# The head of a two-layer decoder trunk: first weights on a second queue, a norm vector spread by products, the second tile's steps reordered

## The chip, the cores and the metric

The kernel runs on one core of one Trainium2 chip. The metric is the device time of one execution in microseconds (us), lower is better. All times and profile rows below are of the kernel before the change, unless said otherwise.

## The reference, cut to what matters

The program computes two layers of a decoder trunk in float32 on 512 positions of 1024 channels. Only the very first sub-layer matters here: the root-mean-square norm of the input, and the product of the result with the value columns of the first mixer's input projection.

```python
def rmsnorm(x, g):
    x32 = x.astype(jnp.float32)
    y = x32 * lax.rsqrt(jnp.mean(x32 * x32, axis=-1, keepdims=True) + EPS)
    return y.astype(x.dtype) * g

h = rmsnorm(x, g_mix_pre[0])
proj = h @ w_in
q, k, v, f_logit, b_gate, c_gate, u = jnp.split(proj, [i1, i2, i3, i4, i5, i6], axis=-1)
...
x = x + rmsnorm(y, g_mix_post[layer])
```

After it come attention, a gated convolution, a recurrent block, two cross attentions and two SwiGLU layers, all untouched by the change.

## The kernel before

**Products.** Each float32 product is made of three passes over float32r operands: both sides are split into a high part (a cast on ScalarE) and a low part (a subtraction on VectorE), and TensorE adds high x high, high x low and low x high. In the tile names, wh and wl are the two parts of a weight tile st, hTh and hTl those of the transposed activations.

**The head of `fox` (lines 1236 to 1325).** The 512 positions are four tiles x[0] to x[3] of 128 rows by 1024 channels. For each tile: `row_stats` (line 235) takes the sum of squares of both halves, `rstd` (line 222) turns it into a factor with two small VectorE operations (L224, L228) and a power on GpSimd (L232), `scaled` (line 253) multiplies tile, factor and norm vector g (L258, two halves h), and `put_T` (line 301) transposes each half with four TensorE instructions into one PSUM bank (L305), casts that bank into hTh (L314, ScalarE) and subtracts it into hTl (L315, VectorE). `mm_v(k0, t, which)` (line 1242) then adds two of the eight 128-channel blocks of tile t into the tile's accumulator: "h" is hTh x wh, "x" is hTl x wh, "w" is hTh x wl; each letter is two matmuls of 512 columns (L1249). The weights come in four loads of 512 KB, `raw[0]`, `raw[2]`, `raw[4]`, `raw[6]`; `whi_v` casts one (L1273, ScalarE), `wlo_v` subtracts it (L1276, VectorE).

**What sets the order.** Inside the `with tc.manual_schedule` block the order of TensorE, ScalarE and VectorE is the order of the program text; each engine works strictly through its own list, and semaphores make it wait. All large loads are issued by SyncE (queue SP), in the order x[0], grow, g1, raw[0], x[1], raw[2], raw[4], x[2], raw[6], x[3].

**The norm vector.** g has two halves. The first is one row, loaded into row 0 of a zeroed tile `grow` and spread over all partitions by a float32 product with a tile of ones (L1280); it stays in a PSUM bank. The second, `g1`, is loaded 128 times over by a broadcasting DMA (L1262). Both are read by `scaled` of all four tiles.

**PSUM.** There are eight banks: pool A's four are the accumulators of the four tiles, pool B's four serve everything else, and a tile takes a bank of its pool when one is free, that is when every instruction on the tile that held it is done:

```python
psA = ctx.enter_context(tc.tile_pool(name="psA", bufs=4, space=bass.MemoryType.PSUM))
psB = ctx.enter_context(tc.tile_pool(name="psB", bufs=4, space=bass.MemoryType.PSUM))
...
for hf in range(2):
    ps = bank()
    for j in range(4):
        nc.tensor.transpose(out=ps[:, j * P:(j + 1) * P], in_=hs[hf][:, j * P:(j + 1) * P], identity=ident)
```

**Filler.** `warm_up(n)` issues n transposes of the identity into a pool-B bank `warm` (L1236); nobody reads them. There are 13 at the start and 4 after L1280.

Of the kernel before, what the change touches and what calls it, by code (L numbers as in the profile page):

```python
# [8 lines left out]
F32 = mybir.dt.float32  # L9
F32R = mybir.dt.float32r  # L10
BF16 = mybir.dt.bfloat16
AF = mybir.ActivationFunctionType
ALU = mybir.AluOpType
PE = mybir.EngineType.PE

P = 128
SEQ = 512
D = 1024
# [5 lines left out]
FOXW = 512  # L24
# [6 lines left out]
WS = 4  # L31
MID = 3
WARM = 13
WARM2 = 4
WHI = 4
WLO = 4
EPS = 1e-6
# [5 lines left out]
def trunk_kernel(ctx: ExitStack, tc: tile.TileContext, a: dict, out: bass.AP):  # L43
# [4 lines left out]
    nc = tc.nc  # L48
# [5 lines left out]
    wst = ctx.enter_context(tc.tile_pool(name="wst", bufs=WS))  # L54
    wlo = ctx.enter_context(tc.tile_pool(name="wlo", bufs=WLO))
    whi = ctx.enter_context(tc.tile_pool(name="whi", bufs=WHI))
    gains = ctx.enter_context(tc.tile_pool(name="gains", bufs=GB))
# [9 lines left out]
    def bankB():  # L67
        return psB.tile([P, 512], F32, tag="B", name="bB")
# [4 lines left out]
    def sbuf(name, n=512):  # L73
        return sp.tile([P, 516], F32, tag="s", name=name)[:, :n]

    def f(ap):
        return ap.bitcast(F32)
# [7 lines left out]
        out=mask, in_=mask, compare_op=ALU.is_ge, fill=1e30, base=0,  # L85
        pattern=[[-1, P]], channel_multiplier=1,
    )
    junk = const.tile([P, 512], BF16, name="junk")
    grow = sbuf("grow")
    ones = sbuf("ones", P)  # L90
    nc.vector.memset(grow, 0.0)
    nc.vector.memset(ones, 1.0)
    nhalf = const.tile([P, 1], F32, name="nhalf")
    nc.gpsimd.memset(nhalf, -0.5)

# [1 line left out]
    x = [xpool.tile([P, D], F32, name=f"x{t}", tag=f"x{t}") for t in range(NT)]  # L97

    def load_x(t):
        nc.sync.dma_start(out=x[t], in_=a["x"][0, t * P:(t + 1) * P, :])  # L100
# [16 lines left out]
    def load_raw(w, k0, nk, c0, c):  # L117
        st = wst.tile([P, nk, c], F32, tag="st", name="st")
        pace(nc.sync.dma_start(
            out=st, in_=w.rearrange("(k p) n -> p k n", p=P)[:, k0:k0 + nk, c0:c0 + c]  # L120
        ))
        return st
# [17 lines left out]
    def pace(load):  # L140

        loads[0] += 1
        if loads[0] > 0 and loads[0] % (COPIES + 1) and copies:
            with tc.issue_after(load.ins):
                copies.pop(0)()
# [73 lines left out]
    def sumsq(src, acc):  # L219
        nc.scalar.activation(out=junk, in_=src, func=AF.Square, accum_out=acc)  # L220

    def rstd(st):

        nc.vector.tensor_scalar(  # L224
            out=st[:, 2:3], in0=st[:, 0:1], scalar1=1.0 / D, scalar2=EPS,
            op0=ALU.mult, op1=ALU.add,
        )
        nc.vector.scalar_tensor_tensor(  # L228
            out=st[:, 3:4], in0=st[:, 1:2], scalar=1.0 / D, in1=st[:, 2:3],
            op0=ALU.mult, op1=ALU.add,  # L230
        )
        pool[0] = nc.gpsimd.tensor_tensor(out=st[:, 4:5], in0=st[:, 3:4], in1=nhalf, op=ALU.pow).ins  # L232
        return st[:, 4:5]

    def stats(name):
        return tiny.tile([P, 8], F32, tag="st", name=name)

    def row_stats(xt, both=False):

        st = stats("pre")  # L240
        for hf in range(2):
            src = xt[:, hf * 512:(hf + 1) * 512]
            if both and hf:
                nc.vector.tensor_tensor_reduce(
                    out=sbuf("sq"), in0=src, in1=src, scale=1.0, scalar=0.0, op0=ALU.mult, op1=ALU.add,
                    accum_out=st[:, hf:hf + 1],
                )
            else:
                sumsq(src, st[:, hf:hf + 1])
        return rstd(st)  # L250
# [36 lines left out]
    def dst_T(hT, hf, t):  # L287
        if hT.hi:
            sl = slice(t * P, (t + 1) * P)
            return hT.ghi[hf][:, :, sl], hT.glo[hf][:, :, sl]  # L290
        q, c = hT.quads[hf][t // 2], t % 2 * P
        return q[:, :, c:c + P], q[:, :, 256 + c:256 + c + P]
# [8 lines left out]
    def put_T(hT, t, hs, bank=bankB):  # L301
# [3 lines that stand above are left out]
                nc.tensor.transpose(  # L305
                    out=ps[:, j * P:(j + 1) * P], in_=hs[hf][:, j * P:(j + 1) * P], identity=ident
                )
            v = ps.rearrange("p (k c) -> p k c", k=4)
            sl = slice(t * P, (t + 1) * P)
            if hT.raw:  # L310
                nc.scalar.copy(out=hT.raw[hf][:, :, sl], in_=v)
            hi, lo = dst_T(hT, hf, t)
            last = (
                nc.scalar.copy(out=hi, in_=v).ins,  # L314
                nc.vector.tensor_tensor(out=lo, in0=v, in1=f(hi), op=ALU.subtract).ins,  # L315
            )
        return last
# [904 lines left out]
    def fox(proj):  # L1222
        w = a["ab_w_in"][0]
# [10 lines left out]
        def warm_up(n):  # L1234
            for _ in range(n):
                nc.tensor.transpose(out=warm[:, 0:P], in_=ident, identity=ident)  # L1236
# [4 lines left out]
        def mm_v(k0, t, which="hxw"):  # L1241

            ts = slice(t * P, (t + 1) * P)
            wh, wl = wv[k0]
            for c in which:
                for kk in range(2):
                    k = k0 + kk
                    passes[t] += 1
                    nc.tensor.matmul(  # L1249
                        out=banks[t], lhsT=(hT.lo if c == "x" else hT.hi)[k][:, ts],  # L1250
                        rhs=(wl if c == "w" else wh)[:, kk, :], start=passes[t] == 1, stop=passes[t] == 3 * KT
                    )
            if passes[t] == 3 * KT:
                dst = vhl[t].rearrange("p (m s d) -> p m s d", s=4, d=64)
                src = banks[t].rearrange("p (m s d) -> p m s d", s=2, d=64)
                split_out(src, dst[:, :, 0::3, :], dst[:, :, 1:3, :])

        with tc.manual_schedule(engines={PE, mybir.EngineType.Activation, mybir.EngineType.DVE}):
            load_x(0)
            nc.sync.dma_start(out=grow[0:1], in_=a["g_mix_pre"][0:1, 0:512])  # L1260
            g1 = gains.tile([P, 512], F32, tag="gain", name="gain")
            nc.sync.dma_start(out=g1, in_=a["g_mix_pre"][0, 512:D].partition_broadcast(P))  # L1262
            raw = {}
            for k0, t in ((0, 1), (2, None), (4, 2), (6, 3)):
                raw[k0] = load_raw(w, k0, 2, 2 * FOXW, 512)
                if t:
                    load_x(t)

            def whi_v(k0):
                hi = whi.tile([P, 2, 512], F32R, tag="wh", name="wh")  # L1270
                lo = wlo.tile([P, 2, 512], F32R, tag="wl", name="wl")
                wv[k0] = hi, lo
                nc.scalar.copy(out=hi, in_=raw[k0])  # L1273

            def wlo_v(k0):
                nc.vector.tensor_tensor(out=wv[k0][1], in0=raw[k0], in1=f(wv[k0][0]), op=ALU.subtract)  # L1276

            nc.scalar.activation(out=junk[:, 0:1], in_=nhalf, func=AF.Square)
            g0 = bankB()
            nc.tensor.matmul(out=g0, lhsT=ones, rhs=grow, start=True, stop=True)  # L1280
            g = g0, g1
            warm_up(WARM2)
            r = row_stats(x[0], True)
            nc.vector.tensor_copy(out=identb, in_=ident)
            hs = scaled(x[0], g, r)
            whi_v(0)
            wlo_v(0)
            put_T(hT, 0, hs)
            mm_v(0, 0, "hwx")
            whi_v(2)  # L1290
            r = row_stats(x[1], True)
            wlo_v(2)
            mm_v(2, 0, "hx")
            hs = scaled(x[1], g, r)
            whi_v(4)
            mm_v(4, 0, "hx")
            put_T(hT, 1, hs)
            mm_v(2, 0, "w")
            r = row_stats(x[2])
            wlo_v(4)  # L1300
            mm_v(0, 1)
            mm_v(2, 1)
            hs = scaled(x[2], g, r)
            whi_v(6)
            wlo_v(6)
            mm_v(4, 1)
            put_T(hT, 2, hs)
            mm_v(4, 0, "w")
            r = row_stats(x[3])
            hs = scaled(x[3], g, r)  # L1310
            mm_v(6, 0)
            mm_v(6, 1)
            for k0 in range(0, KT - 2, 2):
                mm_v(k0, 2)
            put_T(hT, 3, hs)
            mm_v(KT - 2, 2)
            for k0 in range(0, KT, 2):
                mm_v(k0, 3)
# [4 lines left out]
        st = load_raw(w, 0, KT, 3 * FOXW, 32)  # L1323
# [3 lines left out]
        for k in range(KT):  # L1327
# [5 lines left out]
            out=z, in0=ps[0:H], scalar=bf, in1=e, op0=ALU.add, op1=ALU.add  # L1333
# [5 lines left out]
            out=z, in0=z, scalar=0.0, in1=e, op0=ALU.min, op1=ALU.subtract  # L1339
# [3 lines left out]
            out=e, data0=t1, data1=z, initial=0.0, op0=ALU.mult, op1=ALU.add  # L1343
# [305 lines left out]
```

## Time and profile before

| what | value |
|---|---|
| time, median of 3 runs | 1389.0 us (1388.88 the lowest, 5210.49 the highest) |
| the profiled execution's own time | 1390.62 us |
| its span, first to last instruction | 1388.8 us |
| TensorE matmul busy | 1376.7 us, 99% of the span |
| VectorE, ScalarE, GpSimd busy | 1111.4, 727.0, 111.3 us |
| mean granted TensorE clock | 0.997 |

The span is what the rows below divide up; the profiled execution's own time also holds what lies around the span. PE is TensorE's matmuls, PEld its weight loads, DVE VectorE, ACT ScalarE, POOL GpSimd, SP SyncE; a "q" behind a name is the sequencer that issues a DMA. The granted clock (PEclk) is a share of full speed: 1.00 is 2.4 GHz, 0.50 is 1.2 GHz.

### The profile page before, as it was taken

What the parts mean: (1) busy time and instruction counts of PE and PEld (TensorE: products, weight loads), DVE (VectorE), ACT (ScalarE), POOL (GpSimd) and SP (SyncE); (2) the same over time, 40 slices, a digit from 0 to 9 for tenths busy, and PEclk for the clock granted to TensorE, in tenths of its full rate; (3) what the DMA queues carried; (4) which work ended last, traced back from release to release, by engine and by line L of the source; (5) the groups of instructions that cost most, each with busy time, mean ns of one, the idle gap of its engine ahead of it and who ended that gap; (6) DMA issues with size and microseconds to landing.
All of it is one profiled execution on the core that took longest, in us unless ns stands there. A gap on an engine that the chain in (4) does not pass through costs nothing.

```text
span 1388.8 us, 21768 instructions
## 1 busy us (share of the span) xinstructions
PE 1376.7 (99%) x8416; PEld 1226.8 (88%) x8416; DVE 1111.4 (80%) x1801; ACT 727.0 (52%) x1190; POOL 111.3 (8%) x160
## 2 busy tenths in 40 slices
PE   8999999999999999999999999999999999999998
PEld 6778788988899999998889888988889999999886
DVE  5876677645589999989898999653558999999987
ACT  4344456434455444456575797453446444545664
POOL 1000002012010011000001000101200011000001
PEclk9999999999999999999999999999999999999999
DMA  7854452668424566667665657266812555666654
GB/s 225 265 163 147 154 167 76 198 158 167 100 92 133 142 175 170 172 217 233 197 218 180 222 183 240 76 193 159 168 61 92 168 152 156 171 173 232 205 188 144
DMA packets 155250, 233.62 MB, mean 168 GB/s; under 512 B 8477, under 2 KB 90497, under 8 KB 153866
## 3 DMA queue, kind: packets, MB, share of 16 engines
q1 hardware_dynamic: 134562, 179.99, 40.3%
q0 software_dynamic: 17072, 46.16, 15.2%
q10 hardware_dynamic: 3512, 6.08, 1.4%
q8 instruction: 66, 1.08, 0.3%
q14 instruction: 38, 0.31, 0.1%
HBM read 219.60 MB, written 58.74 MB: 200 GB/s over the span
## 4 chain that ended last, share of the span: by engine, by line
PE 95%; issue 3%; DMA 1%; ACT 0%; DVE 0%; POOL 0%; DVEq 0%; SPq 0%; POOLq 0%; ACTq 0%
PE bA L336 13%; PE bA L338 13%; PE bA L337 13%; PE bB L337 6%; PE bB L336 6%; PE bB L338 6%; PE bB L811 3%; PE bB L810 3%; PE bB L812 3%; PE bA L811 2%; PE bA L810 2%; PE bA L812 2%; PE bA L569 2%; PE bA L571 2%; PE bA L570 2%
## 5 line engine op out<-in xcount | busy, mean ns | idle before, releaser
L546 DVE TENSOR_TENSOR wl<-st,wh 128x1024 fp32r<-128x1024 f32 x108 | 131.6, 1222 | 96.6 <-ACT wh L545 95.4
L545 ACT CAST wh<-st 128x1024 fp32r<-128x1024 f32 x108 | 113.1, 1050 | 120.4 <-PE bA L337 70.2
L336 PE MATMUL bA<-hTh,wh 128*128 128x512 f32 (+1 forms) x448 | 171.4, 383 | 0.2 <-ACT hTh L314 0.2
L337 PE MATMUL bA<-hTl,wh 128*128 128x512 f32 (+1 forms) x448 | 167.8, 375 | 0.3 <-DVE hTl L315 0.3
L338 PE MATMUL bA<-hTh,wl 128*128 128x512 f32 (+1 forms) x448 | 168.0, 375 | 0.0
L437 ACT CAST wg<-wr 128x1024 fp32r<-128x1024 f32 x80 | 83.7, 1046 | 49.2 <-DVE wr L466 38.5
L776 ACT CAST wh<-st 128x1024 fp32r<-128x1024 f32 x76 | 74.9, 986 | 63.7 <-PE bA L812 27.0
L338 PEld LDWEIGHTS bA<-hTh,wl 128*128 128x128 f32 x448 | 84.3, 188 | 15.4
L438 DVE TENSOR_TENSOR wg<-wr,wg 128x1024 fp32r<-128x1024 f32 x80 | 97.2, 1215 | 0.0
L337 PEld LDWEIGHTS bA<-hTl,wh 128*128 128x128 f32 x448 | 84.5, 189 | 14.2 <-DVE hTl L315 0.5
L336 PEld LDWEIGHTS bA<-hTh,wh 128*128 128x128 f32 x448 | 84.5, 189 | 14.0 <-ACT hTh L314 0.5
L781 DVE TENSOR_TENSOR wl<-st,wh 128x1024 fp32r<-128x1024 f32 x76 | 86.2, 1134 | 10.1 <-ACT wh L776 10.1
L437 ACT CAST wh<-tt 128x1024 fp32r<-128x1024 f32 x40 | 42.1, 1052 | 61.5 <-DVE tt L466 61.5
L336 PE MATMUL bA<-hTq,wh 128*128 128x256 f32 x208 | 59.2, 284 | 0.0
L338 PE MATMUL bA<-hTq,wl 128*128 128x256 f32 x208 | 58.9, 283 | 0.0
L337 PE MATMUL bA<-hTq,wh 128*128 128x256 f32 x208 | 58.8, 283 | 0.0
L810 PE MATMUL bB<-wh,ya 128*128 128x512 f32 x148 | 57.6, 389 | 0.0
L811 PE MATMUL bB<-wl,ya 128*128 128x512 f32 x148 | 57.6, 389 | 0.0
L812 PE MATMUL bB<-wh,ya 128*128 128x512 f32 x148 | 57.6, 389 | 0.0
L756 DVE TENSOR_TENSOR ya<-yb,ya 128x512 fp32r<-128x512 f32 x84 | 53.4, 639 | 0.0
L810 PE MATMUL bA<-wh,ya 128*128 128x512 f32 x132 | 51.3, 389 | 0.0
L811 PE MATMUL bA<-wl,ya 128*128 128x512 f32 x132 | 51.3, 389 | 0.0
(380 smaller groups left out, 4433.3 us busy)
## 6 DMA issues: line engine op xcount, KB each, us to landing
wr<-in_w_ffn_gu_dram SPq DMA_DIRECT2D x80, 512.0 KB
st<-t SPq DMA_DIRECT2D x40, 512.0 KB
t<-in_w_ffn_down_dram SPq DMA_DIRECT2D x32, 512.0 KB
st<-in_w_xkv_dram SPq DMA_DIRECT2D x32, 512.0 KB
st<-in_w_ffn_down_dram SPq DMA_DIRECT2D x30, 512.0 KB
st<-in_ab_w_in_dram SPq DMA_DIRECT2D x24, 512.0 KB
y<-yr POOLq DMA_DIRECT2D x18, 512.0 KB, 4.1
t<-in_w_ffn_down_dram POOLq DMA_DIRECT2D x16, 512.0 KB, 8.9
```

The source lines that it names most:

```text
L336: nc.tensor.matmul(out=ps, lhsT=wh, rhs=xh, start=first, stop=False)
L337: nc.tensor.matmul(out=ps, lhsT=wh, rhs=xl, start=False, stop=False)
L338: nc.tensor.matmul(out=ps, lhsT=wl, rhs=xh, start=False, stop=last)
L437: return (lambda: nc.scalar.copy(out=to[0], in_=src), lambda: nc.vector.tensor_tensor(out=to[1], in0=src, in1=f(to[0]), op=ALU.subtract))
L438: lambda: nc.vector.tensor_tensor(out=to[1], in0=src, in1=f(to[0]), op=ALU.subtract))
L545: nc.scalar.copy(out=hi, in_=src)
L546: nc.vector.tensor_tensor(out=lo, in0=src, in1=f(hi), op=ALU.subtract)
L776: nc.scalar.copy(out=self.wt[s][0], in_=self.st[s])
L781: nc.vector.tensor_tensor(out=lo, in0=self.st[s], in1=f(hi), op=ALU.subtract)
L810: nc.tensor.matmul(out=banks[t], lhsT=yh, rhs=wh[:, jj, :], start=first and jj == 0, stop=False)
L811: nc.tensor.matmul(out=banks[t], lhsT=yh, rhs=wl[:, jj, :], start=False, stop=False)
L812: nc.tensor.matmul(out=banks[t], lhsT=yl, rhs=wh[:, jj, :], start=False, stop=last and jj == n - 1)
```

## The change

The load of `raw[0]` is issued by ScalarE's queue instead of SyncE's. Both halves of the norm vector are now loaded as single rows (row 0 and row 32 of `grow`), split into a high part `growh` (ScalarE) and a low part `growl` (VectorE), and spread by two float32r products each with `pick`, a tile of zeros and ones; both halves stay in pool-B banks, and the broadcasting load is gone. The ones tile is gone too. The second half of x[1]'s sum of squares moves ahead of `wlo_v(0)` on VectorE, its first half behind `put_T(hT, 0, hs)`, and its `rstd` ahead of `whi_v(2)`. Of the filler, 2 transposes instead of 4 follow the norm vector's products, and 3 new ones stand between `put_T(hT, 0, hs)` and the first `mm_v`. `load_raw`'s pacing hook is bypassed for these four loads; its counter is negative there and set to 0 behind the block.

```diff
--- before.py
+++ after.py
@@ -31,7 +31,8 @@
 WS = 4
 MID = 3
 WARM = 13
-WARM2 = 4
+WARM2 = 2
+WARM3 = 3
 WHI = 4
 WLO = 4
 EPS = 1e-6
@@ -87,9 +88,11 @@
     )
     junk = const.tile([P, 512], BF16, name="junk")
     grow = sbuf("grow")
-    ones = sbuf("ones", P)
+    growh, growl, pick = (gains.tile([P, 512], F32R, tag="gain", name=n) for n in ("growh", "growl", "pick"))
     nc.vector.memset(grow, 0.0)
-    nc.vector.memset(ones, 1.0)
+    nc.vector.memset(f(pick)[:, 0:2 * P], 0.0)
+    for hf in range(2):
+        nc.vector.memset(f(pick)[32 * hf:32 * hf + 1, hf * P:hf * P + P], 1.0)
     nhalf = const.tile([P, 1], F32, name="nhalf")
     nc.gpsimd.memset(nhalf, -0.5)
 
@@ -1257,14 +1260,16 @@
 
         with tc.manual_schedule(engines={PE, mybir.EngineType.Activation, mybir.EngineType.DVE}):
             load_x(0)
-            nc.sync.dma_start(out=grow[0:1], in_=a["g_mix_pre"][0:1, 0:512])
-            g1 = gains.tile([P, 512], F32, tag="gain", name="gain")
-            nc.sync.dma_start(out=g1, in_=a["g_mix_pre"][0, 512:D].partition_broadcast(P))
+            for hf in range(2):
+                nc.sync.dma_start(out=grow[32 * hf:32 * hf + 1], in_=a["g_mix_pre"][0:1, hf * 512:hf * 512 + 512])
+
             raw = {}
-            for k0, t in ((0, 1), (2, None), (4, 2), (6, 3)):
-                raw[k0] = load_raw(w, k0, 2, 2 * FOXW, 512)
+            for k0, engine, t in ((0, nc.scalar, 1), (2, nc.sync, None), (4, nc.sync, 2), (6, nc.sync, 3)):
+                raw[k0] = wst.tile([P, 2, 512], F32, tag="st", name="st")
+                engine.dma_start(out=raw[k0], in_=w.rearrange("(k p) n -> p k n", p=P)[:, k0:k0 + 2, 2 * FOXW:3 * FOXW])
                 if t:
                     load_x(t)
+            nc.scalar.activation(out=junk[:, 0:1], in_=nhalf, func=AF.Square)
 
             def whi_v(k0):
                 hi = whi.tile([P, 2, 512], F32R, tag="wh", name="wh")
@@ -1275,20 +1280,41 @@
             def wlo_v(k0):
                 nc.vector.tensor_tensor(out=wv[k0][1], in0=raw[k0], in1=f(wv[k0][0]), op=ALU.subtract)
 
-            nc.scalar.activation(out=junk[:, 0:1], in_=nhalf, func=AF.Square)
-            g0 = bankB()
-            nc.tensor.matmul(out=g0, lhsT=ones, rhs=grow, start=True, stop=True)
-            g = g0, g1
+
+            nc.scalar.copy(out=growh, in_=grow)
+            g = bankB(), bankB()
+            st = stats("pre")
+
+            def square_v(t, hf):
+                src = x[t][:, hf * 512:(hf + 1) * 512]
+                if hf:
+                    nc.vector.tensor_tensor_reduce(
+                        out=sbuf("sq"), in0=src, in1=src, scale=1.0, scalar=0.0, op0=ALU.mult, op1=ALU.add,
+                        accum_out=st[:, 1:2],
+                    )
+                else:
+                    sumsq(src, st[:, 0:1])
+
+            square_v(0, 1)
+            square_v(0, 0)
+            nc.vector.tensor_tensor(out=growl, in0=grow, in1=f(growh), op=ALU.subtract)
+            r = rstd(st)
+            for hf in range(2):
+                for i, part in enumerate((growh, growl)):
+                    nc.tensor.matmul(out=g[hf], lhsT=pick[:, hf * P:hf * P + P], rhs=part, start=i == 0, stop=i == 1)
             warm_up(WARM2)
-            r = row_stats(x[0], True)
             nc.vector.tensor_copy(out=identb, in_=ident)
             hs = scaled(x[0], g, r)
             whi_v(0)
+            st = stats("pre")
+            square_v(1, 1)
             wlo_v(0)
             put_T(hT, 0, hs)
+            warm_up(WARM3)
+            square_v(1, 0)
             mm_v(0, 0, "hwx")
+            r = rstd(st)
             whi_v(2)
-            r = row_stats(x[1], True)
             wlo_v(2)
             mm_v(2, 0, "hx")
             hs = scaled(x[1], g, r)
```

## Rows read from the trace of the kernel before

**Rows 1.** The page's first part: busy time and share of the span.

```profile
PE 1376.7 (99%) x8416; PEld 1226.8 (88%) x8416; DVE 1111.4 (80%) x1801; ACT 727.0 (52%) x1190; POOL 111.3 (8%) x160
```

**Rows 2.** Waits of TensorE's matmuls over the whole span, the longest three of six.

```profile
PE bA L1249 <- ACT hTh L314: 1.5, 1, 1.5
PE bB L1236 <- POOL ident masks.py:199: 1.5, 1, 1.5
PE bB L305 <- DVE h L258: 1.3, 1, 1.3
```

**Rows 3.** The chain that ended last, first 25 us: start, length, what.

```profile
2.19 7.46 DMA st<-in_ab_w_in_dram
...
11.25 6.27 PE bA L1249 x14
```

**Rows 4.** Timeline of TensorE: start, length, engine, line, tiles, shapes, count.

```profile
1.47 3.03 PE L1236 MATMUL bB<-ident 128*128 128x128 f32 x13 [1.47 <-POOL ident masks.py:199]
4.30 1.91 PE L1280 MATMUL bB<-grow,ones 128*128 128x512 f32 x2
...
7.14 0.66 PE L305 MATMUL bB<-ident,h 128*128 128x128 f32 x4
9.12 0.66 PE L305 MATMUL bB<-ident,h 128*128 128x128 f32 x4 [1.31 <-DVE h L258]
...
14.83 1.06 PE L1249 MATMUL bA<-wh,hTl 128*128 128x512 f32 x2
15.68 1.06 PE L1249 MATMUL bA<-wh,hTh 128*128 128x512 f32 x2
...
17.35 1.04 PE L305 MATMUL bB<-ident,h 128*128 128x128 f32 x8
...
20.39 0.61 PE L1249 MATMUL bA<-wh,hTh 128*128 128x512 f32 x2
20.84 0.62 PE L1249 MATMUL bA<-wh,hTl 128*128 128x512 f32 x2
```

**Rows 5.** Timeline of VectorE, ScalarE and GpSimd, the first tile's chain.

```profile
4.10 0.69 DVE L244 CUSTOM_DVE_ANT_0 sq<-x 128x512 f32<-128x512 f32 x1 [2.56 <-DMA x<-in_x_dram]
4.17 0.63 ACT L220 ACTIVATE junk<-x 128x512 bf16<-128x512 f32 x1 [1.30 <-DMA x<-in_x_dram]
...
5.43 0.56 POOL L232 TENSOR_TENSOR pre<-pre,nhalf 128x1 f32<-128x1 f32 x1 [3.71 <-DVE identb L1284]
...
6.34 0.75 DVE L258 SCALAR_TENSOR_TENSOR h<-x,pre,bB 128x512 f32<-128x512 f32 x1 [0.94 <-PE bB L1280]
...
8.31 0.75 DVE L258 SCALAR_TENSOR_TENSOR h<-x,pre,gain 128x512 f32<-128x512 f32 x1 [1.22 <-DMA gain<-in_g_mix_pre_dram]
...
9.67 1.04 ACT L1273 CAST wh<-st 128x1024 fp32r<-128x1024 f32 x1 [4.78 <-DMA st<-in_ab_w_in_dram]
10.62 1.07 ACT L314 CAST hTh<-bB 128x512 fp32r<-128x512 f32 x2
10.74 1.23 DVE L1276 TENSOR_TENSOR wl<-st,wh 128x1024 fp32r<-128x1024 f32 x1 [1.68 <-ACT wh L1273]
...
11.88 1.28 DVE L315 TENSOR_TENSOR hTl<-bB,hTh 128x512 fp32r<-128x512 f32 x2
...
13.08 0.68 DVE L244 CUSTOM_DVE_ANT_0 sq<-x 128x512 f32<-128x512 f32 x1
```

**Rows 6.** Windows: stretch, length, busy by engine, granted clock, DMA share, GB/s.

```profile
2.00:4.00 2.00, 2.00 (x11) 2.00 (x10) 0.00 (x0) 0.85 (x2) 0.00 (x0) 1.00 1.05 283
4.00:6.00 2.00, 2.00 (x5) 0.86 (x4) 1.15 (x5) 0.72 (x2) 0.56 (x1) 1.00 0.76 102
...
7.10:10.40 3.30, 1.31 (x8) 0.84 (x8) 0.75 (x1) 0.73 (x1) 0.00 (x0) 1.00 1.02 400
10.60:17.20 6.60, 5.95 (x14) 4.65 (x15) 5.74 (x10) 3.69 (x7) 1.47 (x1) 0.50 1.07 374
17.40:25.00 7.60, 7.57 (x41) 5.79 (x40) 5.43 (x9) 4.52 (x10) 1.46 (x1) 1.00 0.70 217
```

## The prediction

> **What bounds the kernel now.** I read the page's busy shares first: TensorE works 1376.7 us of the 1388.8 us span [rows 1], so only its idle time and its slow time can be won. The list of its waits says where the idle time is: 1.5 us before the first filler, 1.3 us before the second group of transposes, 1.5 us before the first V matmul, each once [rows 2]; the other three of that list are shorter. All three lie in the first 11.25 us. So whatever moves the point from which TensorE runs dense moves the end by as much, and nothing later swallows it. The chain of waits names what holds that point: the load of raw[0], from its issue at 2.19 to its landing at 9.65 [rows 3], then its cast on ScalarE (9.67, 1.04 us), the cast of the first hTh behind it on the same engine (10.62) [rows 5], and 14 matmuls from 11.25 on [rows 3]. Then I asked for the granted clock by stretches: 1.00 until 10.4, 0.50 from 10.6 to 17.2, 1.00 from 17.4 on [rows 6]; 0.50 is 1.2 GHz, 1.00 is 2.4 GHz. A pair of matmuls starts every 0.85 us in the slow stretch and every 0.45 us behind it [rows 4], 0.43 and 0.225 us a matmul. The first clock rows need care: fillers at 1.47 take 3.03/13 = 0.23 us each, the transposes at 17.35 take 1.04/8 = 0.13 [rows 4], so TensorE began at the low level whatever the 1.00 in the rows 2 to 6 us says.
>
> **Where I measure.** All 14 matmuls of the first tile (six of `mm_v(0, 0)`, four of `mm_v(2, 0)`, four of `mm_v(4, 0)`) stand ahead of the second tile's transposes in both kernels. Those start at 17.35 [rows 4]. I work out when they start after the change and call the difference the effect.
>
> **Loads.** The change removes the 128-fold load of g1, during which the DMA engines were 0.76 busy and moved only 102 GB/s from 4 to 6 us [rows 6], and takes raw[0] out of SP's row, where x[0], grow and g1 stood before it. In SP's row two rows of grow now stand between x[0] and x[1]. raw[0] and x[0] are then under way together. x[0] lands at 4.10 now [rows 5]. It can stay there (0), or wait until raw[0] is through as well: 0.52 MB more at 283 GB/s [rows 6] is 5.95 (+1.85). Below 0 I see nothing, as g1 stood behind it. I take 4.6 (+0.5), nearer to the low end, since half of x[0] is through before raw[0] starts. raw[0] lands near 5.95 (behind x[0] alone) or as late as 7.8 (x[1]'s 0.52 MB through first); x[1] between 6.7 (1.05 MB behind x[0] at 400 GB/s [rows 6]) and 8.7 (that and half of raw[2] at 283).
>
> The Trainium skill, "DMA: Bandwidth & Descriptors", section "Issuing engines are not separate DMA queues", speaks against this part: loads started by several engines share the same 16 DMA engines, and only issue time is saved. By that rule alone x[0] would be at the late end, and the sum below 0.7 us larger; the DMA share of 1.05 from 2 to 4 us [rows 6] agrees that there is no spare engine.
>
> **The norm vector.** Added: a cast of 128x512 on ScalarE, 1.07/2 = 0.53 us by the cast of hTh; a subtraction on VectorE, 1.28/2 = 0.64 by hTl [rows 5]; four products of 512 columns at 0.43. Gone: two products of L1280, 1.91 together [rows 4], and the wait of the second h for g1, 1.22 [rows 5]. On ScalarE the cast comes before the sum of squares: 4.6 + 0.53 + 0.63 = 5.76 (the row of grow may land up to 0.5 later or with x[0]; I take with it). From the end of that sum (4.80 now) to the power is 0.63, the power 0.56 [rows 5], so the factor is there at 6.95 and the two h run 7.0 to 7.75 and 7.75 to 8.5, against 9.06 now. growl is ready at 4.6 + 0.7 + 0.64 = 5.95, so the first half's product ends about 6.4, the second's at 7.3, and both are hidden; the cover is thin (0.45 us before the second h).
>
> **The first tile, where the gain is given back.** The old kernel had four pool-B banks for warm, g's first half and the first tile's two transposed halves. Now warm is still needed by the three new fillers behind `put_T`, and g holds two banks to the end of the block. One bank is left. The second half's transposes must wait until the first half has been cast and subtracted out of that bank, and that subtraction (hTl) is behind other work in VectorE's list: the second h (ends 8.5), the moved square of x[1] (0.68, to 9.2), `wlo_v(0)` (1.23, to 10.45; its cast is through by then, as raw[0] need only land by 8.1), hTl itself 0.64: 11.1. Queued behind the waiting transposes on TensorE is everything else. The first half's own transposes end near 8.7, so TensorE idles 2.4 us. From 11.1: four transposes and three fillers at 0.23 are 1.6 us, and the first V matmul starts at 12.7 (12.0 if they ran at 0.13), 1.45 us later than now. Everything that it needs is there, and raw[2]'s cast and the second tile's h (about 17) come in time.
>
> **The clock.** The dense stretch begins at 11.1 instead of 11.25, with the same kind of pause before it, so I leave the fall near 10.5 and the rise at 17.3. By 17.3, (17.3 - 12.7)/0.43 = 10.7 matmuls are through; the other 3.3 take 0.75 us: the second tile's transposes start at 18.05, 0.7 us later than now. (While the rise stays put, 1 us of later start costs only about 0.5, since what is lost was slow time.) Bounds: with x[0] at 4.10, start 12.2, +0.45; with x[0] at 5.95, start 14.05, +1.4.
>
> **The other edits.** x[1]'s moved halves and its `rstd` are the same instructions; their price is the 0.68 us above. Memsets on VectorE lie before x[0] lands. Two fillers fewer, three more: counted above. Behind 18.05 the lists are unchanged, and the later tiles' inputs come sooner than now: 0.
>
> **Sum.** The profiled execution takes 1390.62 (its span 1388.8 and 1.8 around it); plus 0.7 is 1391.3. It lies 1.6 above the median of the runs shown, so against that 1389.0 the forecast is 1389.7.
>
> **Rivals.**
> First, the bank doesn't block (a bank comes free that I count as held). For it: three new fillers in front of the first matmul would have a pause to fill only then. Against it: pool B has four banks and three have later readers. Then the second transposes run at 8.5 to 9.4, the fillers to 10.1, hTh is ready, low parts follow VectorE (wl 10.45, hTl 11.1), and TensorE is dense from 7.8 and so keeps the high level. The 14 matmuls then go at the pace of ScalarE's casts: raw[4]'s cast ends near 13, and the second h of x[1] near 15.2, so the transposes start around 15.1: -2.2 us, 1386.8.
> Second, the bank blocks but the clock rises earlier, near 14, the seven short instructions counting as part of the dense stretch. For it: the same short ones stood before the high level at 7.1. Against it: ahead of the last rise TensorE had been busy 5.95 of 6.60 us [rows 6], and the new dense stretch is no older at 14. Three matmuls slow and eleven at 0.225: transposes at 16.45, -0.9, 1388.1.
> The Trainium skill, "TensorE: Matmul & The Clock Gate", section "Part 4: PE-mode transpose", says that transposes don't count as busy work for the clock in the same way. By that rule this rival is out and 1389.7 stands; the fall of the clock behind a stretch that held only eight transposes, 1.31 us of 3.30 [rows 6], agrees, but no row has them dense and alone.
> Third, on the slow side: x[1] lands late. Its square now stands ahead of `wlo_v(0)` and hTl, so from a landing at 8.5 on each microsecond delays the blocked transposes by one. The trace bounds the landing by 13.08, where its square ran without a wait [rows 5]. Halfway, 10.8, the first matmul starts at 15.0 and the transposes at 19.2: +1.9, 1390.9; at the bound +3, 1392. For it: three loads now share the start. Against it: g1's slow stretch is gone.
>
> **How the numbers follow.** Forecast 0.5, bank free 0.2, earlier clock 0.18, late x[1] 0.12. The likeliest one's own range is 1389.1 to 1390.7 (the bounds of x[0], a little either side). To hold 8 in 10 over both signs I go from 1386.6 (first rival) to 1391.3 (third rival's nearer half). A measurement of this kernel can tell about 2%, 28 us, from no change; all idle and slow time of the head together is under 10 us, so same 0.98, and 0.01 for each side for a reordering elsewhere that I don't see.
>
> **What would show it.** Right: the second group of L305 starts 2 us or more after the first and is released by L315; L1249 starts near 12.7; the clock is 0.50 to about 17.3; raw[0]'s cast no longer waits for its load. Wrong: both groups of L305 lie together and L1249 starts at 10 to 11 (first rival); 1.00 from 14 on (second); L244's second instance waits for x (third).

## The result, and the profile after

| kernel | median, us | runs | ratio to before, 95% interval |
|---|---|---|---|
| before | 1389.25 | 17 | |
| after | 1391.99 | 17 | 1.0020 (1.0013 to 1.0028) |

The change costs 2.74 us. The forecast was +0.7 us, 1389.7, with a range up to 1391.3: the sign is right, the size is too small, and the time lies 0.7 us above the range. The profiled execution of after took 1392.30 us, its span is 1390.5, 1.7 more than before's.

The page's first line shows that TensorE is as busy as before over a longer span [rows 1], so the time went into waits or slow work:

```profile
PE 1376.0 (99%) x8419; PEld 1226.6 (88%) x8419; DVE 1112.4 (80%) x1804; ACT 727.4 (52%) x1191; POOL 110.2 (8%) x160
```

The waits of TensorE's matmuls, the longest four (in total, times, longest), beside [rows 2]:

```profile
PE bB L1304 <- ACT growh L1284: 2.3, 1, 2.3
PE bB L308 <- DVE hTl L318: 2.0, 1, 2.0
PE bB L1239 <- POOL ident masks.py:199: 1.5, 1, 1.5
PE bA L308 <- DVE h L261: 1.0, 1, 1.0
```

The second is the blocked bank of the forecast: transposes into pool B (bB) that wait for hTl. The first is the norm vector's row, the fourth was forecast by nobody: it writes a pool-A bank (bA), so it is not in the head at all, where pool A holds the accumulators. The chain that ended last tells the head in one piece (start, length, what), in the place of [rows 3]:

```profile
1.79 4.27 DMA grow<-in_g_mix_pre_dram
...
6.17 0.63 ACT growh L1284
...
6.81 0.69 DVE growl L1300
...
7.94 0.56 POOL pre L235
...
8.53 0.75 DVE h L261 x2
...
9.91 0.69 DVE sq L1291
...
10.60 1.14 DVE wl L1281
11.74 0.61 DVE hTl L318
...
12.40 0.66 PE bB L308 x4
13.06 0.33 PE bB L1239 x3
13.39 4.79 PE bA L1252 x14
```

Before, this chain ran through raw[0] and ScalarE; now it runs from the row of grow through VectorE: the second h, the moved square, raw[0]'s subtraction, hTl, and only then the second half's transposes, the three fillers and the 14 matmuls. TensorE's timeline, beside [rows 4], gives the points of the forecast:

```profile
9.43 0.96 PE L308 MATMUL bB<-ident,h 128*128 128x128 f32 x4
12.40 0.66 PE L308 MATMUL bB<-ident,h 128*128 128x128 f32 x4 [2.01 <-DVE hTl L318]
...
13.14 0.83 PE L1252 MATMUL bA<-wh,hTh 128*128 128x512 f32 x2
...
18.02 1.03 PE L308 MATMUL bB<-ident,h 128*128 128x128 f32 x8
```

First matmul at 13.14 (forecast 12.7, before 11.25), second tile's transposes at 18.02 (forecast 18.05, before 17.35). That last agreement is in part luck: the blocked transposes start 1.3 us later than forecast (12.40 against 11.1), but they and the three fillers take 0.74 us instead of the 1.6 of the forecast, and the low clock has ended by 17.0. Windows of the granted clock, beside [rows 6]:

```profile
13.60:16.90 3.30, 3.30 (x10) 2.38 (x9) 2.56 (x5) 2.58 (x5) 0.55 (x1) 0.50 0.61 180
17.00:20.00 3.00, 3.00 (x17) 2.12 (x16) 1.54 (x4) 1.35 (x3) 0.00 (x0) 1.00 0.79 248
```

So the head of these two executions differs by 0.67 us, but their spans by 1.7. The missing 1.0 us is the fourth wait, at the transposes of a later projection (timeline of TensorE, after):

```profile
232.28 0.39 PE L574 MATMUL bB<-rh,y 128*128 128x512 f32 x1
233.63 1.29 PE L308 MATMUL bA<-ident,h 128*128 128x128 f32 x8 [0.97 <-DVE h L261]
```

There VectorE was held by an hTl that waited for the store of memT, 1 MB that GpSimd sends to memory:

```profile
DVE hTl L318: 1.5, 1
...
DMA to landing us min/median/max: 6.1/6.1/6.1
```

### The profile page after: what moved, and what is told of

Read it like the earlier page. It is cut to its first block, busy times and chain, and to the rows that moved or that the text cites. A ratio compares the mean times of both kernels' runs of the same rounds, so it can differ in the third digit from the quotient of the medians.

```text
span 1390.5 us, 21779 instructions
## 1 busy us (share of the span) xinstructions
PE 1376.0 (99%) x8419; PEld 1226.6 (88%) x8419; DVE 1112.4 (80%) x1804; ACT 727.4 (52%) x1191; POOL 110.2 (8%) x160
## 4 chain that ended last, share of the span: by engine, by line
PE 94%; issue 3%; DMA 1%; DVE 1%; ACT 0%; POOL 0%; DVEq 0%; ACTq 0%; POOLq 0%; SPq 0%
PE bA L339 13%; PE bA L341 13%; PE bA L340 13%; PE bB L339 6%; PE bB L340 6%; PE bB L341 6%; PE bB L815 3%; PE bB L813 3%; PE bB L814 3%; PE bA L815 2%; PE bA L813 2%; PE bA L814 2%; PE bA L572 2%; PE bA L574 2%; PE bA L573 2%
```

## The experiments

My theory was now: (A) the loss is a blocked bank behind a late row, plus (B) an accident at 232 us. Every kernel was timed beside the kernel before, and each profile also shows the store of memT. The medians of the kernel before lie between 1389.19 and 1389.76 in these rounds, so a difference of two medians from different rounds is good to about half a microsecond; the same difference by the ratios to before is given beside it where it matters.

**The late wait: fewer fillers after, more before.** `fill10` and `before_fill16` change one constant, the number of fillers at the start. In the kernel after, TensorE idles behind them; in the kernel before, three more push the norm vector's product back, and yet the second tile's transposes start no later (15.71, against 17.35 in [rows 4]).

```diff
-WARM = 13
+WARM = 10
```
```diff
-WARM = 13
+WARM = 16
```

> The kernel after the change with 10 instead of 13 fillers at the start, where TensorE idles 2.3 us anyway. Theory A (late fetch): the 0.97 us wait of the transposes at 232.7 us comes from the store of memT sharing a DMA engine with a fetch of TensorE's instructions; three instruction pairs fewer let that fetch come about 0.7 us later, behind the store's tail. Then the wait is gone or much smaller, the head is as before, and the time is about 1 us less, 1391.0. Rival (the store is slow by itself, or by load traffic): the wait stays at about 1 us and the time at 1392.0.

> The kernel before the change with 16 instead of 13 fillers at the start. In the head they delay the norm vector's product by about 0.7 us, which the second h hides, as it waits for g1 until 8.3. Theory A (late fetch): three instruction pairs more bring the fetch of TensorE's instructions into the store of memT, a wait of about 1 us appears at the transposes near 232 us, 1390.3. Rival: nothing changes, 1389.3.

fill10: 1390.92 (ratio to before 1.0008, 0.9999 to 1.0016), 1.07 under after, 1.7 by the ratios. before_fill16: 1391.17 (1.0008, 0.9999 to 1.0017), 1.4 over the kernel before beside it, 1.1 by the ratio, whose interval only just holds no change; its profile has the new wait, 1.0 us for DVE h at the same transposes. What decides is in the DMA view of the same 4.1 us from the store's issue on; first after, then fill10:

```profile
q0 software_dynamic: 140, 1.02, 61.7%
q8 instruction: 1, 0.02, 1.5%
```
```profile
q0 software_dynamic: 143, 1.05, 62.8%
```

In after a 16 KB fetch of instructions falls into that stretch, and 140 packets of the store have started by its end; in fill10 the fetch comes later, 143 have started, and the store, issued at 224.8 as against 224.7, lands in 4.8 instead of 6.1 us:

```profile
DVE hTl L318: 0.2, 1
...
DMA to landing us min/median/max: 4.8/4.8/4.8
```

The same split runs through all fourteen profiles: the seven of programs with 8419 matmuls have a landing of 6.0 to 6.3 us, the seven of programs with 8416 one of 4.8 or 4.9. The change's three extra TensorE instruction pairs moved the fetch forward into the store. The packet records of the traces say more. In the seven profiles with the short landing the fetch starts 2 or 3 ns after the store's last packet ends. In the other seven it starts 1.9 to 4.6 us before that end, and the store's last packets end one after another, 0.31 us apart. That fits one DMA engine which both have to pass, though the records do not name the engine, nor whose instructions are fetched.

**The bank.** `bank_free` lets the three new fillers write a pool-A bank that is reset later, so warm's bank is free.

```diff
-            warm_up(WARM3)
+            warm_up(WARM3, banks[NT - 1])
```

> The kernel after the change, its three new fillers written into the last accumulator bank of pool A, so that the bank of warm is free for the first tile's second transposes. Theory (bank): the second group of transposes no longer waits for hTl but follows the second h at about 10.0, the first V matmul starts near 11.5 instead of 13.1, and the time is 0.8 to 1.6 us less, 1390.4 to 1391.2 (the wait near 232 us may stay). Rival (the low parts on VectorE hold the matmuls anyway): the transposes move but the second tile's transposes don't, and the time stays at 1392.

1390.26 (1.0005, 0.9996 to 1.0013), 1.73 under after, 2.1 by the ratios. All eight transposes now go in one piece, and the first matmul starts 1.8 us earlier (timeline of TensorE):

```profile
9.15 1.92 PE L308 MATMUL bB<-ident,h 128*128 128x128 f32 x8
...
11.36 1.06 PE L1252 MATMUL bA<-wh,hTh 128*128 128x512 f32 x2
```

**The bank and the fetch together.** `bank_fill10` is bank_free with `WARM = 10`.

> bank_free with 10 instead of 13 fillers at the start: the blocked bank and the late fetch repaired together, nothing else. Theory (the two are the whole loss): 1.7 and 1.1 us add up, 1389.1 to 1389.4, the same as the kernel before, with no wait near 232. Rival (the head's gain of bank_free is taken back by the wait near 75 us, or a third loss is left): 1389.8 or more.

1388.84 (ratio to before 0.9994, 0.9985 to 1.0002): 3.15 under after, 3.6 by the ratios, and no different from before. The two repairs account for the whole loss; what else the change does is too small to be told from nothing here. The wait near 75 us is 0.3 us, as in after; in bank_free it was 0.7.

**The row.** `grow_act` issues the two rows on ScalarE's queue, ahead of raw[0]; `raw0_sp` leaves them and takes raw[0] back to SyncE's queue.

```diff
-                nc.sync.dma_start(out=grow[32 * hf:32 * hf + 1], ...
+                nc.scalar.dma_start(out=grow[32 * hf:32 * hf + 1], ...
```
```diff
-            for k0, engine, t in ((0, nc.scalar, 1), (2, nc.sync, None), ...
+            for k0, engine, t in ((0, nc.sync, 1), (2, nc.sync, None), ...
```

> The kernel after the change, the two rows of the norm vector loaded over ScalarE's queue ahead of raw[0] instead of over SyncE's behind x[0]. Theory (late row): the rows land before x[0], the factor is ready 1.4 us earlier, both h, the blocked transposes and the first V matmul move by 1.4 us (13.1 to 11.7), and the time is 0.7 to 1.4 us less, 1390.6 to 1391.3. Rival (the bank alone decides, or x[0] lands later for it): less than 0.3 us.

> The kernel after the change with raw[0] on SyncE's queue, behind the norm vector's rows, instead of on ScalarE's: the second queue alone undone. Theory (order of issue decides the landings, whatever the queue): the rows land near 4.3 instead of 6.1, since only x[0] is issued ahead of them, raw[0] near 5.6; both h, the blocked transposes and the first V matmul move 1.6 to 1.9 us ahead, and the time is 0.9 to 1.9 us under after_again. Rival (a row on one DMA engine is late by itself): less than 0.4 us.

grow_act missed: 1393.49, 1.5 over after. The rows came 0.7 us earlier, not 2, and raw[0] fell far back (timeline of ScalarE and TensorE; the brackets hold the idle time before and what ended it):

```profile
5.46 0.62 ACT L1284 CAST growh<-grow 128x512 fp32r<-128x512 f32 x1 [1.46 <-DMA grow<-in_g_mix_pre_dram]
...
10.12 1.04 ACT L1278 CAST wh<-st 128x1024 fp32r<-128x1024 f32 x1 [3.42 <-DMA st<-in_ab_w_in_dram]
...
13.08 1.11 PE L308 MATMUL bB<-ident,h 128*128 128x128 f32 x4 [3.33 <-DVE hTl L318]
```

With the rows waiting for grow's memset on ScalarE, raw[0] was issued behind x[1] and raw[2] of SyncE's queue, and being on another queue did not bring it ahead of them.

raw0_sp missed too: 1392.26, the same as after_again (1391.97). The rows are early, as expected, yet the blocked transposes start only 0.5 us earlier (0.3 against after_again), because another input is now later (timeline):

```profile
4.47 0.62 ACT L1284 CAST growh<-grow 128x512 fp32r<-128x512 f32 x1 [1.61 <-DMA grow<-in_g_mix_pre_dram]
...
8.07 1.04 ACT L1278 CAST wh<-st 128x1024 fp32r<-128x1024 f32 x1 [2.36 <-DMA st<-in_ab_w_in_dram]
...
9.38 0.69 DVE L1291 CUSTOM_DVE_ANT_0 sq<-x 128x512 f32<-128x512 f32 x1 [1.13 <-DMA x<-in_x_dram]
...
11.88 1.12 PE L308 MATMUL bB<-ident,h 128*128 128x128 f32 x4 [3.57 <-DVE hTl L318]
```

That is the third rival's mechanism: x[1] lands late, VectorE waits 1.13 us for it, and its square stands ahead of the hTl that frees the bank. raw[0] is later too, but its cast is done by 9.11, before the subtraction needs it. By the landings in the traces the second queue does bring raw[0] and x[1] sooner, at 6.55 and 7.85 in after against 8.05 and 9.36 in raw0_sp; its price is the row, at 6.06 against 4.37.

**The same kernel again.**

> The kernel after the change as it is, to have its time beside the following ones and the kernel before on one chip, and a second profile. Both theories: about 2.7 us over before; in the profile the norm vector's rows land near 6.1, the second transposes wait for hTl until about 12.4, and a wait of about 1 us stands near 232.7 again.

1391.97 (1.0021, 1.0012 to 1.0030), 2.8 over the 1389.19 of before beside it: the loss repeats. The store lands in 6.0 us here, again with a wait of 0.9 behind it.

**The order of the second tile.** `order_back` puts the square, the factor and raw[2]'s cast back where they were.

```diff
-            st = stats("pre")
-            square_v(1, 1)
             wlo_v(0)
             put_T(hT, 0, hs)
             warm_up(WARM3)
-            square_v(1, 0)
             mm_v(0, 0, "hwx")
-            r = rstd(st)
             whi_v(2)
+            r = row_stats(x[1], True)
             wlo_v(2)
```

> The kernel after the change with the second tile's square, its factor and raw[2]'s cast in the order of before, so that nothing stands between the second h and raw[0]'s subtraction on VectorE. Theory (the square delays the hTl that frees the bank): the blocked transposes start 0.6 to 0.7 us earlier (11.7), the time is 0.3 to 0.7 us under after_again. Rival (the order is neutral): 0 to 0.2 us.

1391.95, no gain. The blocked transposes do start at 11.71 instead of 12.40 (12.17 in after_again), but the second tile's h comes no earlier (16.52 against 16.41 in after), and TensorE stops twice (timeline of TensorE):

```profile
15.54 0.73 PE L1252 MATMUL bA<-wh,hTh 128*128 128x512 f32 x2 [0.36 <-ACT wh L1278]
...
17.41 1.22 PE L308 MATMUL bB<-ident,h 128*128 128x128 f32 x8 [0.67 <-DVE h L261]
```

**All repairs, and all without the bank's.** `all_three` joins raw0_sp, the fillers in pool A, order_back and `WARM = 10`; `no_bank` is the same with the fillers in warm.

> The kernel after the change with all repairs at once: raw[0] on SyncE's queue behind the rows, the three fillers in pool A's last bank, the second tile's order of before, 10 fillers at the start. Theory: the second transposes follow the second h near 8.4, the first V matmul starts at 9.3 to 10, 1.3 to 2 us ahead of the kernel before, and the time is 1 to 2 us under before, 3.5 to 4.5 under after_again, less what the wait near 75 us (0.7 in bank_free against 0.3) takes back. Rival (the early head is swallowed there and by the fetch): no better than before.

> all_three without the bank's repair: the three fillers are written into warm's bank again. Theory (bank): the second transposes wait for hTl until about 10.6, the first V matmul starts near 11.9 instead of 9.9, and the time is 1 to 2 us over all_three, 1389.3 to 1390.2. Rival (the other repairs carry the gain): within 0.4 us of all_three.

all_three: 1388.20 (0.9994, 0.9985 to 1.0002), 3.8 under after_again; against before the interval just reaches no change. no_bank: 1390.06 (1.0002, 0.9993 to 1.0011), 1.9 more by the medians and 1.1 by the ratios (the kernel before stood at 1389.7 beside no_bank). The difference by the ratios is no wider than their intervals, so the times alone don't settle that the bank counts here too; the wait shows it. In no_bank the second transposes start at 11.0, released by hTl after a wait of 2.4.

**A version that beats both.** `late_low` is all_three with the second tile's sum of squares ahead of raw[2]'s cast, and raw[2]'s subtraction behind the second tile's h.

```diff
+            r = row_stats(x[1], True)
             whi_v(2)
-            r = row_stats(x[1], True)
-            wlo_v(2)
             mm_v(2, 0, "hx")
             hs = scaled(x[1], g, r)
+            wlo_v(2)
```

> all_three with the second tile's sum of squares ahead of raw[2]'s cast on ScalarE and raw[2]'s subtraction behind the second tile's h on VectorE, so that GpSimd's power does not run beside that subtraction (1.47 us there, 0.55 without). Theory: the second tile's h starts near 12.7 instead of 13.9, its transposes at 13.5 to 14.0 instead of 14.8, and the time is 0.5 to 1 us under all_three, 1387.2 to 1387.7, under the kernel before by more than its interval. Rival (TensorE's own matmuls set that point): less than 0.3 us.

1387.26 (0.9983, 0.9974 to 0.9992): faster than before by more than the interval, 2.4 us, and 4.7 under after. GpSimd's power and what follows, all_three and then late_low (timeline):

```profile
12.40 1.47 POOL L235 TENSOR_TENSOR pre<-pre,nhalf 128x1 f32<-128x1 f32 x1 [5.66 <-DVE pre L231]
...
14.79 1.29 PE L308 MATMUL bB<-ident,h 128*128 128x128 f32 x8 [0.67 <-DVE h L261]
```
```profile
12.14 0.55 POOL L235 TENSOR_TENSOR pre<-pre,nhalf 128x1 f32<-128x1 f32 x1 [5.51 <-DVE pre L231]
...
13.90 1.04 PE L308 MATMUL bB<-ident,h 128*128 128x128 f32 x8
```

**The kernel before, again.**

> The kernel before the change as it is: a second profile, to see whether the granted clock rises at the same point of the head again (17.3 in the first one, whose execution was 1.4 us above the median of its kernel). Theory (the rise lies elsewhere in each execution): it rises earlier here, the second tile's transposes start 1 to 2 us before 17.35, and the execution's own time is nearer to 1389.2. Rival (the rise is tied to the program): 17.3 again, time 1390.6.

Profiled execution 1389.22 us, span 1387.5; median 1390.19 (1.0001, 0.9992 to 1.0010). The program is the same, the head is not (windows, then TensorE's timeline):

```profile
13.60:16.90 3.30, 2.62 (x16) 1.73 (x14) 2.32 (x3) 0.71 (x2) 1.32 (x1) 1.00 1.10 362
```
```profile
10.25 1.22 PE L1249 MATMUL bA<-wh,hTh 128*128 128x512 f32 x2 [1.66 <-ACT hTh L314]
...
15.84 1.29 PE L305 MATMUL bB<-ident,h 128*128 128x128 f32 x8 [0.64 <-DVE h L258]
```

The clock is high here where it was low in the first profile [rows 6], and the second tile's transposes start at 15.84, not 17.35 [rows 4]. This shift of 1.5 us is the difference of the two spans to within 0.2 (1388.8 and 1387.5). The clock is not its only cause: raw[0] was there 1.0 us sooner as well, so that its cast starts at 8.66 instead of 9.67 [rows 5] (timeline of ScalarE):

```profile
8.66 1.04 ACT L1273 CAST wh<-st 128x1024 fp32r<-128x1024 f32 x1 [3.74 <-DMA st<-in_ab_w_in_dram]
```

The h that releases the second tile's transposes stands behind that load's subtraction in VectorE's list, and it too came 1.0 us sooner (14.95 against 15.94). With the late load it would have held them to about 16.8 whatever the clock did. So about 1.0 us of the shift is the load's and about 0.5 the clock's: an estimate from these rows. The first profile was one of the slowest executions of its kernel (of 126 on record, 8 took 1390.62 or more), and I had worked out the change from it alone. The same transposes in before_fill16, in after_again and in fill10 (timelines of TensorE):

```profile
15.71 1.29 PE L305 MATMUL bB<-ident,h 128*128 128x128 f32 x8 [0.17 <-DVE h L258]
```
```profile
17.76 1.03 PE L308 MATMUL bB<-ident,h 128*128 128x128 f32 x8
```
```profile
18.26 1.03 PE L308 MATMUL bB<-ident,h 128*128 128x128 f32 x8
```

## Why the prediction was wrong in size

- **The blocked bank: right.** Transposes released by hTl, TensorE idle 2.0 us (2.4 forecast), the first matmul 1.9 us later than in [rows 3] (1.45 forecast). Freeing the bank is worth 1.73 us by itself, 2.1 with the late wait gone (fill10 to bank_fill10), 1.1 to 1.9 in all_three. The first rival is out.
- **The base of the sum, and the clock in it: the step that failed in the head.** I left "the fall near 10.5 and the rise at 17.3", counted from the 17.35 of one profile, and then took the 1.6 us by which that execution lay above its median off both kernels alike. Nearly all of the 1.6 lies in the head of before, in that execution: its load of raw[0] and the end of its low clock (17.3, but by 13.6 in before_again) were both late. The three profiles with the head of before have the second tile's transposes at 16.3 on average (17.35, 15.84, 15.71), the three with that of after at 18.0 (18.02, 17.76, 18.26). So the head costs about 1.7 us, an estimate from few profiles, instead of 0.7. The medians agree, 2.74 - 1.07 = 1.7 (by the ratios of fill10 it is 1.1). My 18.05 for after holds, in part by luck, as said above. What a microsecond of later start costs is not settled: freeing the bank moved the first matmul by 1.8 us and the second tile's transposes by 2.7 (18.02 to 15.31), while from before_again to after the same two points move by 2.9 and 2.2.
- **"Behind 18.05 the lists are unchanged", a term of 0: failed.** The lists are, but three TensorE instruction pairs more moved an instruction fetch into the store of memT. From the second tile's transposes to the end of the span it is 1371.5 and 1371.7 us in the two profiles of before and 1371.2 in fill10, but 1372.5 and 1372.4 in after and after_again. So a term of about 1 us stood at nothing (1.07 by the medians, 1.7 by the ratios); fill10 and before_fill16 show its wait go and come. No rival had a place behind the head.
- **The row of grow: mis-sized.** I let it land with x[0]; x[0]'s square started at 4.75 and the row's cast at 6.17, so the factor was 1.5 us later than forecast (6.95 against 8.49). The 4.6 for x[0] itself was about right (it lands at 4.72), and so were the bounds for raw[0] and x[1] (6.55 and 7.85). Whether the late row cost anything on balance stays open: in raw0_sp, with the row early, x[1] is late, and the blocked transposes hardly move.
- **The second tile's order: priced at 0.68, worth 0.** It does delay the bank by 0.7, and without it TensorE stops for 0.36 and 0.67 later on (order_back).
- **The second rival** (an earlier rise) is not a mechanism of the change: the low stretch ended by 17.0 in after, and the rise lay differently in executions of one and the same program. For the same reason the rule of the Trainium skill ("TensorE: Matmul & The Clock Gate", "Part 4: PE-mode transpose"), that transposes don't count as busy work for the clock in the same way, could not be told from its opposite. The third rival didn't occur in after, where x[1]'s square ran without a wait at 9.91; it did in raw0_sp.

The forecast of no change at the level of 2% holds.

## What to carry to other kernels

Count the banks of a pool with the last reader of each tile, not the writers: here three fillers that nobody reads kept a bank, made TensorE wait 2.0 us for another, and cost 1.1 to 2.1 us of the kernel's time. When a profiled execution lies off the median of its kernel by as much as the effect, find out where in the span the excess lies, with a second profile, before taking it off the forecast. And a change of a few instructions can act far behind its place: here three pairs in the head, more or fewer, moved an instruction fetch into a store and out of it again, 230 us later.

## What was not expected of the hardware

- A 16 KB instruction fetch during a 1 MB store stretched its landing from 4.8 or 4.9 to between 6.0 and 6.3 us, in seven of fourteen profiles, exactly those of the programs with 8419 matmuls.
- Two loads of one 2 KB row, issued by 2.0 us, were both there only at 6.1 us behind two 512 KB loads issued ahead of them on two queues (after), and at 4.4 behind one (raw0_sp). On another queue, issued behind two such loads, both were there at 5.4 (grow_act). No run separates the order of issue from the queue.
- GpSimd's power on 128 values took 1.47 us while VectorE subtracted a 128x1024 tile, and 0.55 otherwise (late_low).
